# Scores pair by pair of heads, a search traced by an estimate, and decays from rows of sums: one change to a hybrid attention block

## The chip, the cores and the metric

The kernel runs on one core of a Trainium2 chip. The time is that of one execution on the device in microseconds. TensorE multiplies matrices, VectorE, ScalarE and GpSimd work elementwise, and SyncE issues the transfers. PSUM is the memory into which TensorE accumulates.

## The reference, cut to what matters

One residual block over 1024 rows of 1024 columns: a mixer of two parallel head groups, one output projection, and an MLP. One input projection makes everything that the mixer needs.

```python
def hybrid_mixer(h, w_in, ...):
    proj = h @ w_in
    q_a, c_kv, q_idx, k_idx, w_idx, q_b, k_b, v_b, a_b, b_b, z_b = jnp.split(proj, ...)
    o_a = dsa_mixer(q_a, c_kv, q_idx, k_idx, w_idx, ...)
    o_b = gated_deltanet_mixer(q_b, k_b, v_b, a_b, b_b, z_b, ...)
    return jnp.concatenate([o_a, o_b], axis=-1) @ w_out

# dsa_mixer, for a block of 128 rows: 8 index heads score all keys, the 256 best are kept
    rel = jax.nn.relu(jnp.einsum('bqhd,bsd->bqhs', qi_b, k_idx))
    score = jnp.einsum('bqhs,bqh->bqs', rel, wi_b)
    score = jnp.where(key_pos < limit, score, -jnp.inf)
    _, idx = lax.top_k(score, topk)

# gated delta rule, for a chunk of 64 rows, one of 4 heads
    g = jnp.cumsum(chunks(g), axis=-1)
    decay = jnp.exp(jnp.where(causal, g[..., :, None] - g[..., None, :], -jnp.inf))
    lower = jnp.where(strict, jnp.einsum('bhncd,bhnsd->bhncs', k_beta, k) * decay, 0.0)
    intra = jnp.where(causal, jnp.einsum('bhncd,bhnsd->bhncs', q, k) * decay, 0.0)
```

## The kernel before

The input projection is a loop over 26 tiles of 128 columns. Each is 48 matmuls: two halves of 512 rows, eight slices of the inner sum, and three products of a high and a low part (lines L199, L200, L201). The columns come in this order: keys and weights of the index heads (kw), four tiles of index queries (qi, a pair of heads in each), then keys and queries of the delta heads in turn (kb, qb), vb, z, the latents c and the attention's queries (qa). A tile's result in PSUM is called two.

What follows a tile is in `projections()`. Behind kw come the gates of the delta rule and, for each of eight blocks of 128 rows, `decays(n)`: two matmuls that sum the gates' logarithms, one exponential, a triangle on GpSimd, and a write to memory (tile tmp, tensor e_d). Behind the fourth qi come the scores, block after block. For each slice of at most 512 keys and each of 8 heads, two matmuls (L480, L481) go to a PSUM bank called tr or ch, ScalarE takes the relu (L486), and VectorE adds it, weighted, to the tile score (L484, L487). Only blocks 7 to 2 are scored: the first two blocks have no more than 256 keys.

The search for the 256th best score, `bisect()`, is 32 steps of counting how many scores lie below a candidate, three blocks on VectorE (L527) and three on ScalarE (L521), with small operations between (L530 to L532). Then masks are made on VectorE (L569 to L577, tile maskb). The convolutions of kb, qb and vb are three multiply-adds on VectorE each (L587, tile tmp). `delta_head(h)` builds the triangular systems of a head (last product L701, tile la). The latents are normalized by two products (L451, L452, tile c_row), turned by TensorE and copied (L1096, tile CT). The attention also needs the up-projection as a split copy (L1088, tile UK).

The order is made by a planner, `Flow`. It holds generators and estimates when each engine and each ring of buffers is free; a generator yields the time or the event that it waits for, and the one that can go on earliest issues next. The search is no part of it in the kernel before: `projections()` advances it by a fixed number of steps after each tile (the table rate). Every engine works through its own queue in the order of issue.

Of the kernel before, what the change touches and what calls it, by code (L numbers as in the profile page):

```python
# [8 lines left out]
F32 = mybir.dt.float32  # L9
# [130 lines left out]
def block_kernel(ctx: ExitStack, tc: tile.TileContext, x, w_in, c_norm, w_uk, w_uv, rel_bias, conv_w, a_log,  # L140
# [98 lines left out]
    after_r = pl.t(dc, [P, P], F32R, "after_r")  # L239
# [49 lines left out]
    warmr = pl.t(px, [P, 1024], F32R, "warmr")  # L289
    V.memset(warmr.bitcast(F32), 0.0)  # L290
    ps = psw()
    for _ in range(10):
        PE.matmul(ps[:, 0:512], warm[:, 0:P], warm, start=True, stop=True)
    ps = psw()
    two = warmr[:, 0:512].rearrange("p (a b) -> p b a", a=2)
    forms = [(warmr[:, 0:P], two), (warmr[:, 0:P], warmr[:, 0:512].rearrange("p (a b) -> p b a", a=4)),
             (warmr[:, 0:256:2], two), (warmr[:, 0:P], warmr[:, 0:256].rearrange("p (a b) -> p b a", a=2))]
    for lhs, rhs in forms:
        o = ps[:, 0:rhs.shape[1] * rhs.shape[2]].rearrange("p (a b) -> p a b", b=rhs.shape[2])
        for _ in range(4):  # L300
            PE.matmul(o, lhs, rhs, start=True, stop=True)
    for _ in range(4):
        for r in range(2):
            rs = slice(64 * r, 64 * r + 64)
            PE.matmul(ps[:, 512 * r:512 * r + 512].rearrange("p (b a) -> p b a", a=2), warmr[rs, 0:P], two[rs],
                      start=True, stop=True)
# [65 lines left out]
    la_d = pl.t(dram, [P, NB * 4, 2, P], F32, "la_d")  # L372
    e_d = pl.t(dram, [4, P, NB, P], F32, "e_d")
# [101 lines left out]
    def scores(b):  # L475
        for s0, w in cuts(P * (b + 1)):
            dst = score[:, soff[b] + s0:soff[b] + s0 + w]
            for h in range(8):
                ps = psx()
                PE.matmul(ps[:, :w], QS[:, h, b * P:(b + 1) * P], KH[:, s0:s0 + w], start=True, stop=False)  # L480
                PE.matmul(ps[:, :w], QS[:, h, b * P:(b + 1) * P], KL[:, s0:s0 + w], start=False, stop=True)  # L481
                wh = wab[:, b, h:h + 1]
                if h == 0:
                    V.tensor_scalar(dst, ps[:, :w], 0.0, wh, op0=OP.max, op1=OP.mult)  # L484
                else:
                    S.activation(ps[:, :w], ps[:, :w], AF.Relu)  # L486
                    V.scalar_tensor_tensor(dst, ps[:, :w], wh, dst, op0=OP.mult, op1=OP.add)  # L487
        G.memset(score[0:64, soff[b] + P * b + 64:soff[b] + P * (b + 1)], PAD)
# [8 lines left out]
    def bisect():  # L497

# [17 lines left out]
        for bit in range(31, -1, -1):  # L516
            flip = (1 << bit) ^ (1 << (bit - 1)) if bit else 1
            for i, b in enumerate(ACB):
                n = P * (b + 1)
                junk = pl.t(ph, [P, T], BF16, "jk", bufs=2)  # L520
                S.activation(junk[:, :n], s_of(b), AF.Sign, bias=cand[:, 3 + i:4 + i].bitcast(F32), scale=-1.0,  # L521
                             accum_out=cnt[:, 3 + i:4 + i])
            for i, b in enumerate(DVB):
                n = P * (b + 1)
                junk = pl.t(ph, [P, T], BF16, "pre")
# [12 lines left out]
            yield  # L538
# [6 lines left out]
        for i, b in enumerate(ACB):  # L545
# [8 lines left out]
            yield  # L554
# [5 lines left out]
        for b in range(NB - 1, 1, -1):  # L560
# [17 lines left out]
            yield  # L578
# [41 lines left out]
    gpr = pl.t(keep, [P, 2, NB, 4], F32R, "gp")  # L620
    gp = gpr.bitcast(F32)

    def gates():
# [32 lines left out]

    def decays(n):

        ps = psx()
        gms = pl.t(ph, [P, 2, 4, P], F32R, "tmp", bufs=4)  # L660
        for i in range(2):
            gm = gms[:, i]
# [287 lines left out]
    def projections():  # L950
        nonlocal dna, dn, dn_close
        for i, (kind, p) in enumerate(plan):
# [19 lines left out]
            if kind == "kw":  # L972
# [3 lines left out]
                for n in range(NB):  # L976
                    decays(n)
# [824 lines left out]
```

## Time and profile before

| | |
|---|---|
| time, median of 3 runs (lowest to highest) | 1409.54 us (1406.29 to 1410.04) |
| profiled execution | 1411.07 us, span 1409.4 us |
| granted TensorE clock, mean | 0.955 |
| TensorE, VectorE, ScalarE, GpSimd busy | 1298.3, 1104.0, 729.7, 271.1 us |

The span is the profiled execution from its first to its last instruction on the core. Busy time counts what an engine executes and not its waits for another. In rows, x2 behind an operation means two of them in one row, an arrow `<-` in brackets names what ended the idle time ahead of an instruction, and L201 is line 201 of the kernel of that run. The profile's shares are means over stages with different limits, so the stages are read one by one.

### The profile page before, as it was taken

To read this page: it belongs to the slowest core of one execution; us is meant where nothing else is said; L and a number is where in the kernel's file an instruction comes from. 1 tells how busy PE (TensorE), PEld (TensorE's weight loads), DVE (VectorE), ACT (ScalarE), POOL (GpSimd) and SP (SyncE) were. 2 spreads that over 40 slices of the span, in tenths; PEclk is the share of its full clock that TensorE was granted. 3 is DMA by queue.
4 is the path that set the end of the run, shared out by engine and by line. 5 is a ranking of instruction groups with operands and counts; after the bars stand their busy time and mean duration, and the time that the engine had idled before them with its cause. 6 is when DMAs were issued, how large, how long until landed. Compare 5 with 4: busy or idle time off the path is not lost.

```text
span 1409.4 us, 20293 instructions
## 1 busy us (share of the span) xinstructions
PE 1298.3 (92%) x6643; PEld 1119.7 (79%) x6643; DVE 1104.0 (78%) x2551; ACT 729.7 (52%) x1521; POOL 271.1 (19%) x296
## 2 busy tenths in 40 slices
PE   7898997998886999999899889999999799999995
PEld 4687895777675799997788778888888688888884
DVE  5524668999999698898777387777777987878886
ACT  4333336768651577677546456565566332343422
POOL 3154221121215345337410000000000000000023
PEclk7999998999995799999999999999999999999998
DMA  6133112456225433333456744555556966646215
GB/s 192 47 97 82 30 46 60 120 149 162 63 70 139 135 89 97 103 110 123 124 171 200 260 158 179 210 206 203 199 206 234 379 237 240 233 126 217 76 50 175
DMA packets 183523, 211.24 MB, mean 150 GB/s; under 512 B 28081, under 2 KB 123514, under 8 KB 183290
## 3 DMA queue, kind: packets, MB, share of 16 engines
q1 hardware_dynamic: 183418, 209.94, 46.2%
q8 instruction: 53, 0.87, 0.3%
q14 instruction: 52, 0.43, 0.1%
HBM read 136.48 MB, written 74.99 MB: 150 GB/s over the span
## 4 chain that ended last, share of the span: by engine, by line
PE 66%; DVE 19%; DMA 6%; ACT 5%; issue 2%; SPq 1%; DVEq 0%; ACTq 0%
PE ch L201 4%; PE sc L199 4%; PE acc L200 4%; PE acc L199 4%; PE sc L201 4%; PE sc L200 4%; PE ch L199 4%; PE acc L201 4%; PE ch L200 4%; PE two L199 4%; PE two L200 4%; PE two L201 4%; DVE pre L527 2%; PE tr L199 2%; PE tr L200 2%
## 5 line engine op out<-in xcount | busy, mean ns | idle before, releaser
L199 PE MATMUL two<-hTH,wh 128*128 128x512 f32 (+1 forms) x416 | 166.9, 403 | 26.0 <-ACT tmp L424 16.0
L200 PE MATMUL two<-hTL,wh 128*128 128x512 f32 (+1 forms) x416 | 166.3, 400 | 0.0
L201 PE MATMUL two<-hTH,wl 128*128 128x512 f32 (+1 forms) x416 | 165.4, 398 | 0.0
L1759 POOL TENSOR_TENSOR tmp<-acc,c_row 128x512 f32<-128x512 f32 x16 | 20.7, 1301 | 635.2 <-DVE acc L1772 626.4
L199 PEld LDWEIGHTS two<-hTH,wh 128*128 128x128 f32 (+1 forms) x416 | 82.3, 198 | 43.3 <-issue 22.6
L521 ACT ACTIVATE jk<-score,cand 128x1024 bf16<-128x1024 f32 (+2 forms) x96 | 92.4, 964 | 45.0 <-DVE cand L532 26.8
L201 PEld LDWEIGHTS two<-hTH,wl 128*128 128x128 f32 (+1 forms) x416 | 81.9, 197 | 12.8 <-issue 1.0
L200 PEld LDWEIGHTS two<-hTL,wh 128*128 128x128 f32 (+1 forms) x416 | 81.9, 197 | 12.3 <-issue 0.7
L1422 ACT CAST hl<-raw 128x512 fp32r<-128x512 f32 x81 | 48.5, 614 | 72.9 <-PE acc L200 48.0
L1422 ACT CAST hl<-tt 128x512 fp32r<-128x512 f32 x56 | 34.4, 617 | 72.6 <-PE tr L200 44.3
L270 POOL TENSOR_TENSOR wl<-stg,wh 128x1024 fp32r<-128x1024 f32 (+1 forms) x26 | 60.8, 2340 | 55.5 <-ACT wh L267 54.0
L1422 ACT CAST hl<-tmp 128x512 fp32r<-128x512 f32 x60 | 35.8, 617 | 55.8 <-DVE tmp L1539 30.4
L1423 DVE TENSOR_TENSOR hl<-raw,hl 128x512 fp32r<-128x512 f32 x81 | 55.7, 692 | 6.3 <-PE acc L201 3.4
L1158 ACT ACTIVATE big<-big,nm 128x256 f32<-128x256 f32 (+6 forms) x64 | 50.6, 791 | 13.5 <-DVE nm L1157 13.5
L269 POOL TENSOR_SCALAR wh<-stg 128x1024 fp32r<-128x1024 f32 x19 | 20.1, 1058 | 190.4 <-PE two L200 190.4
L1183 ACT CAST part<-tr 128x512 fp32r<-128x512 f32 x80 | 43.2, 543 | 21.9 <-PE tr L1181 18.3
L1184 DVE TENSOR_TENSOR part<-tr,part 128x512 fp32r<-128x512 f32 x80 | 50.3, 631 | 4.8 <-ACT part L1183 4.4
L1206 PE MATMUL acc<-part,VS 128*128 128x256 f32 x288 | 49.4, 295 | 1.3 <-DVE part L1184 1.0
L1134 POOL TENSOR_TENSOR mt<-tz,maskb 128x256 f32<-128x256 f32 x56 | 37.8, 679 | 60.2 <-DVE mx L1150 39.7
L587 DVE SCALAR_TENSOR_TENSOR tmp<-two,svT,tmp 128x1023 f32<-128x1023 f32 (+2 forms) x36 | 45.5, 1276 | 4.1 <-ACT tmp L585 3.0
L199 PE MATMUL sc<-hl,hq 128*128 128x512 f32 x112 | 43.3, 386 | 5.2 <-DMA hq<-hid 2.4
L201 PE MATMUL ch<-h2H,hl 128*128 128x512 f32 x112 | 43.6, 390 | 3.6 <-DVE hl L1423 3.6
(516 smaller groups left out, 4159.2 us busy)
## 6 DMA issues: line engine op xcount, KB each, us to landing
hid<-tmp SPq DMA_DIRECT2D x140, 256.0 KB, 2.3
hq<-hid SPq DMA_DIRECT2D x80, 256.0 KB, 5.2
raw<-in_w_mlp_in_dram SPq DMA_DIRECT2D x14, 1024.0 KB, 5.5
tmp<-hid SPq DMA_DIRECT2D x56, 256.0 KB, 5.3
raw<-in_w_mlp_out_dram SPq DMA_DIRECT2D x13, 1024.0 KB, 8.5
stg<-in_w_in_dram SPq DMA_DIRECT2D x25, 512.0 KB, 4.0
x<-in_x_dram SPq DMA_DIRECT2D x8, 512.0 KB, 5.3
la_d<-la SPq DMA_DIRECT2D x8, 512.0 KB, 3.7
```

Source lines behind the costliest of these rows:

```text
L199: PE.matmul(o, lh, rh, start=start, stop=False, skip_group_check=more)
L200: PE.matmul(o, lh, rl, start=False, stop=False, skip_group_check=more)
L201: PE.matmul(o, ll, rh, start=False, stop=stop, skip_group_check=more)
L270: G.tensor_sub(wl[:, :, :n], f[:, :, :n], wh[:, :, :n].bitcast(F32))
L521: S.activation(junk[:, :n], s_of(b), AF.Sign, bias=cand[:, 3 + i:4 + i].bitcast(F32), scale=-1.0, accum_out=cnt[:, 3 + i:4 + i])
L587: V.scalar_tensor_tensor(acc[:, 3 - j:T], both[:, 0:T - 3 + j], w[j], acc[:, 3 - j:T], op0=OP.mult, op1=OP.add)
L1158: S.activation(pr[:, :n], pr[:, :n], AF.Exp, bias=nm, accum_out=den[:, hh:hh + 1])
L1183: S.copy(pt[:, 0:2 * nj, 0, :], v4(ps)[:, 0:2 * nj])
L1184: V.tensor_sub(pt[:, 0:2 * nj, 1, :], v4(ps)[:, 0:2 * nj], pt[:, 0:2 * nj, 0, :].bitcast(F32))
L1206: PE.matmul(po[:, hh * 256:hh * 256 + 256], VS[:, j + a, 2 * p + hh, :], pt[:, 2 * a + hh].rearrange("p a t -> p (a t)"), start=j + a + hh ...
L1422: S.copy(h_, src)
L1423: eng.tensor_sub(l_, src, h_.bitcast(F32))
```

## The change

It has four parts.

- The warm-up of TensorE before the first transposes is 34 matmuls of one kind in place of 10 of that kind and 24 of four other forms.
- The scores become a generator of the planner, `scoring()`. It goes pair by pair of heads, as each qi tile is done, and over all blocks for that pair, and waits for an estimated free PSUM bank. The low part of a block's last columns is filled behind all scores.
- The search becomes a generator too, which begins at the event "scored" and yields an estimate of each step's time; the table of rates goes. The other generators' estimates are changed with it.
- The decays: the gates' running sums (32 columns, a block and head each) are copied, negated (ng), transposed on TensorE to 32 rows, and written to memory (g_d). For two blocks at a time one transfer spreads eight rows of g_d to all 128 partitions, GpSimd puts -1e30 outside the triangle, and ScalarE takes eight exponentials of 128 columns each, with the negated sum as its bias. The four calls stand behind the first kb tile and the first qb tile and not behind kw.

```diff
     ps = psw()
-    for _ in range(10):
+    for _ in range(34):
         PE.matmul(ps[:, 0:512], warm[:, 0:P], warm, start=True, stop=True)
...
-    def scores(b):
-        for s0, w in cuts(P * (b + 1)):
-            dst = score[:, soff[b] + s0:soff[b] + s0 + w]
-            for h in range(8):
...
+    def scoring():
+        for p in range(4):
+            yield ("qi", p)
+            for b in range(NB - 1, 1, -1):
+                for s0, w in cuts(P * (b + 1)):
+                    dst = score[:, soff[b] + s0:soff[b] + s0 + w]
+                    for h in (2 * p, 2 * p + 1):
+                        while flow.bank("px", 4) > flow.now:
+                            yield flow.bank("px", 4)
+                        ps = psx()
...
+                        t = flow.pe(2 * w / 2260)
...
+                        flow.took("px", dve(t, w / 960 + 0.16))
+                        yield 0.0
...
+        flow.done("scored", flow.rings["px"][-1])
...
     def bisect():
+        yield "scored"
...
+            ta = td = flow.now
...
+                ta = act(ta, n / 1200 + 0.45)
...
+                td = dve(td, n / 960 + 0.28)
...
-            yield
+            yield dve(max(ta, td), 0.8)
...
-        S.copy(gpr[:, 0], g)
-        V.tensor_sub(gpr[:, 1], g, gp[:, 0])
-        S.copy(after_r, after)
...
+        V.tensor_copy(gs, ps[:, 0:32])
+        V.tensor_scalar(sm("ng", (P, 32)), gs, -1.0, None, op0=OP.mult)
+        PE.transpose(ps[0:32, 128:256], gs, ident)
+        gt = pl.t(ph, [32, P], F32, "gt")
+        V.tensor_copy(gt, ps[0:32, 128:256])
+        SY.dma_start(g_d, gt)
 
     def decays(n):
-        for i in range(2):
-            gm = gms[:, i]
-            G.tensor_tensor(gm, upto[:, None, :].to_broadcast(H4), b4(gp[:, i, n, :]), OP.mult)
-            PE.matmul(ps, after_r, gm.rearrange("p h c -> p (h c)"), start=i == 0, stop=i == 1)
-        S.activation(e, v4(ps), AF.Exp)
-        G.affine_select(e, e, pattern=[[0, 4], [1, P]], compare_op=OP.is_ge, fill=0.0, base=0, channel_multiplier=-1)
-        SY.dma_start(e_d[:, :, n, :].rearrange("h s c -> s h c"), e)
+        e = tmp4()
+        src = g_d[4 * n:4 * n + 8, :]
+        SY.dma_start(e, bass.AP(tensor=src.tensor, offset=src.offset, ap=[[0, P], [1, T]]))
+        G.affine_select(e3, e3, pattern=[[0, 8], [1, P]], compare_op=OP.is_ge, fill=-1e30, base=0,
+                        channel_multiplier=-1)
+        for i in range(8):
+            S.activation(e[:, cs], e[:, cs], AF.Exp, bias=sm("ng", (P, 32))[:, 4 * n + i:4 * n + i + 1])
+        for i in range(2):
+            SY.dma_start(e_d[:, :, n + i, :].rearrange("h s c -> s h c"), e3[:, 4 * i:4 * i + 4])
...
-                for n in range(NB):
-                    decays(n)
-            elif (kind, p) == ("qi", 3):
-                for b in range(NB - 1, 1, -1):
-                    scores(b)
...
-            for _ in range(rate.get(kind, 0)):
-                next(topk, None)
...
-    for rank, gen in enumerate((chain(), levels(0), levels(1), emits(), projections())):
+    for rank, gen in enumerate((chain(), levels(0), levels(1), emits(), scoring(), bisect(), projections())):
```

TensorE's queue around the first score. In the kernel before it stands behind 305 matmuls of projections (L199 to L201), in the seventh tile, next to the last decay (L664); ident, hTH, hTL, wh and wl are operands of transposes and projections, KH, KL and QS the split keys and the queries of the index heads:

```order
L199 MATMUL two_1384<-hTH_108,wh_820 128x512
L200 MATMUL two_1384<-hTL_109,wh_820 128x512
L664 MATMUL tr_611<-tmp_612,after_r_84 128x512
L480 MATMUL tr_883<-KH_377,QS_376 128x512
L481 MATMUL tr_883<-KL_378,QS_376 128x512
L201 MATMUL two_1384<-hTH_108,wl_821 128x512
```

In the changed kernel the scores' matmuls are L471 and L472, and the first two pairs stand behind 120 of the projections:

```order
L200 MATMUL two_621<-hTL_108,wh_391 128x512
L201 MATMUL two_621<-hTH_107,wl_392 128x512
L471 MATMUL ch_641<-KH_374,QS_373 128x512
L472 MATMUL ch_641<-KL_375,QS_373 128x512
L471 MATMUL ch_650<-KH_374,QS_373 128x512
L472 MATMUL ch_650<-KL_375,QS_373 128x512
L199 MATMUL two_774<-hTH_107,wh_552 128x512
```

What moved: the first score, from the seventh tile to the end of the second tile's first half. The last score stands behind 624 projection matmuls before, and behind 524 in the changed kernel.

ScalarE's queue where the decays' exponentials begin. Before, one of them (L666) stands between copies of the index queries (L409) and a split copy of weights (L267):

```order
L409 ACTIVATE QS_376<-two_763 64x512
L666 ACTIVATE tmp_557<-tr_551 128x512
L409 ACTIVATE QS_376<-two_763 64x512
L267 CAST wh_757<-stg_759 128x1024
L409 ACTIVATE QS_376<-two_700 64x512
```

In the changed kernel (copies L394, relus of the scores L478, exponentials L671, x8 is eight in a row):

```order
L478 ACTIVATE ch_674<-ch_674 128x448
L394 ACTIVATE QS_373<-two_621 64x512
L394 ACTIVATE QS_373<-two_774 64x512
L671 ACTIVATE tmp_1288<-tmp_1288,sm_ng_501 128x128 x8
L478 ACTIVATE ch_686<-ch_686 128x384
L671 ACTIVATE tmp_1303<-tmp_1303,sm_ng_501 128x128 x8
L478 ACTIVATE ch_702<-ch_702 128x384
```

What moved: the exponentials come in groups of eight, and relus of scores stand between and behind them.

VectorE's queue where the latents are normalized. Before, both products stand among steps of the search (L527, L530) and products of the triangular systems (L720, L721):

```order
L451 TENSOR_TENSOR c_row_355<-c_row_355,cr_y_3223 128x1024
L527 TENSOR_SCALAR pre_3274,cnt_1347<-score_372,cand_1345 128x896
L530 TENSOR_SCALAR bare_1346<-cand_1345 128x6
L721 TENSOR_TENSOR kqh_2242<-kqh_2242,kqh_2247 128x6x26
L452 TENSOR_TENSOR c_row_355<-c_row_355,cn_b_3199 128x1024
```

In the changed kernel they (L436, L437) stand behind the last mask (L578), and behind the small steps of a reciprocal root (L215 to L217):

```order
L578 TENSOR_SCALAR maskb_352<-jk_3635 128x384
L215 SCALAR_TENSOR_TENSOR cr_u_2941<-cr_y_2940 128x8
L216 TENSOR_TENSOR cr_u_2941<-cr_u_2941,css_2918 128x8
L217 SCALAR_TENSOR_TENSOR cr_y_2940<-cr_u_2941,cr_y_2940 128x8
L436 TENSOR_TENSOR c_row_351<-c_row_351,cr_y_2940 128x1024
L437 TENSOR_TENSOR c_row_351<-c_row_351,cn_b_2916 128x1024
```

What moved: the normalization, from the middle of the search to the end of the masks. Between the last score and the fourth delta head's last row, VectorE's queue holds 21 operations of convolutions (L587) in place of 18, and 16 of each of the search's small operations in place of 17; TensorE's holds 341 to 365 projection matmuls in place of 312.

## Rows read from the trace of the kernel before

**Rows 1.** The page: busy time of three engines (share of the span, instructions), and the chain that ended last by engine.

```profile
PE 1298.3 (92%) x6643; PEld 1119.7 (79%) x6643; DVE 1104.0 (78%) x2551; ACT 729.7 (52%) x1521; POOL 271.1 (19%) x296
...
PE 66%; DVE 19%; DMA 6%; ACT 5%; issue 2%; SPq 1%; DVEq 0%; ACTq 0%
```

**Rows 2.** Busy time by stretch: the stretch and its length, then busy us (and instructions) of TensorE, its weight loads, VectorE, ScalarE and GpSimd, the granted clock, and the share and rate of transfers.

```profile
0.00:70.70 70.70, 54.26 (x229) 37.98 (x229) 39.56 (x75) 31.34 (x51) 16.99 (x63) 0.83 0.41 119
70.70:115.80 45.10, 44.76 (x209) 38.74 (x208) 11.01 (x21) 15.24 (x25) 29.11 (x26) 1.00 0.34 92
115.80:230.00 114.20, 107.79 (x492) 89.79 (x490) 74.24 (x102) 50.12 (x90) 29.49 (x26) 0.97 0.19 50
230.00:341.90 111.90, 95.28 (x429) 80.11 (x428) 108.52 (x297) 80.73 (x158) 22.26 (x16) 0.92 0.43 123
341.90:457.20 115.30, 90.13 (x404) 76.86 (x404) 110.21 (x268) 56.74 (x128) 32.90 (x20) 0.83 0.41 106
457.20:676.00 218.80, 210.06 (x1627) 191.10 (x1628) 188.88 (x719) 154.17 (x408) 101.45 (x114) 0.96 0.36 108
```

**Rows 3.** Timeline of TensorE: the 119th and 120th matmul of the projections. Columns here and below: start, duration, engine, line, operation, out<-in, shape, count, and idle time ahead with its releaser.

```profile
70.48 0.38 PE L200 MATMUL two<-hTL,wh 128*128 128x512 f32 x1
70.70 0.38 PE L201 MATMUL two<-hTH,wl 128*128 128x512 f32 x1
```

**Rows 4.** Timeline of TensorE around the first score.

```profile
114.03 0.38 PE L200 MATMUL two<-hTL,wh 128*128 128x512 f32 x1
114.25 0.38 PE L201 MATMUL two<-hTH,wl 128*128 128x512 f32 x1
114.46 0.38 PE L199 MATMUL two<-hTH,wh 128*128 128x512 f32 x1
114.68 0.38 PE L200 MATMUL two<-hTL,wh 128*128 128x512 f32 x1
114.89 0.40 PE L664 MATMUL tr<-tmp,after_r 128*128 128x512 f32 x1
115.13 0.40 PE L480 MATMUL tr<-KH,QS 128*128 128x512 f32 x1
115.37 0.40 PE L481 MATMUL tr<-KL,QS 128*128 128x512 f32 x1
```

**Rows 5.** Timelines of VectorE: the last weighted score, the last row of the fourth delta head, the last mask.

```profile
229.42 0.62 DVE L487 SCALAR_TENSOR_TENSOR score<-ch,wab,score 128x384 f32<-128x384 f32 x1
...
341.44 0.47 DVE L701 SCALAR_TENSOR_TENSOR la<-ch,sm_f,eh 128x256 f32<-128x256 f32 x1
...
456.26 0.93 DVE L577 TENSOR_SCALAR maskb<-jk 128x384 bf16<-128x384 bf16 x1
```

**Rows 6.** Waits: engine, tile and line that waited <- what released it, then us in total, times, longest. The first two are VectorE's from 70.7 to 229.5 us, the last two TensorE's from 229.5 to 341.5 us.

```profile
DVE QS L410 <- ACT QS L409: 27.8, 10, 10.1
DVE score L487 <- ACT ch L486: 23.6, 17, 6.5
...
PE tr L700 <- DVE la L701: 6.6, 3, 3.3
PE two L199 <- DVE tmp L587: 3.7, 1, 3.7
```

**Rows 7.** The decays' operations by line (duration in ns: least, median, most; first and last start), the landing of their writes, the exponential of the gates' sums, a 128-column activation of the attention, and two transfers of 512 KB on the page (KB each, median us from issue to landing).

```profile
L666 ACT ACTIVATE tmp<-tr x4: 578/590/597, 78.3 to 116.5; 128x512 f32<-128x512 f32 x4
...
L663 POOL TENSOR_TENSOR tmp<-upto,gp x16: 1033/1040/1054, 73.4 to 117.0; 128x512 fp32r<-128x512 f32 x16
...
L667 POOL TENSOR_SCALAR_AFFINE_SELECT tmp<-tmp x8: 628/634/647, 78.9 to 123.7; 128x512 f32<-128x512 f32 x8
...
DMA to landing us min/median/max: 2.3/2.3/4.1
...
76.38 0.25 ACT L655 ACTIVATE sm_eg<-tr 128x96 f32<-128x96 f32 x1 [0.66 <-PE tr L653]
...
462.56 0.30 ACT L923 ACTIVATE sq<-o 128x128 bf16<-128x128 f32 x1
...
stg<-in_w_in_dram SPq DMA_DIRECT2D x25, 512.0 KB, 4.0
...
x<-in_x_dram SPq DMA_DIRECT2D x8, 512.0 KB, 5.3
```

**Rows 8.** The page: the convolutions' multiply-adds (busy us, mean ns of one | idle ahead of them).

```profile
L587 DVE SCALAR_TENSOR_TENSOR tmp<-two,svT,tmp 128x1023 f32<-128x1023 f32 (+2 forms) x36 | 45.5, 1276 | 4.1 <-ACT tmp L585 3.0
```

**Rows 9.** Timelines: the latents' normalization on VectorE, then ScalarE's copies of the latents and of the up-projection.

```profile
401.35 1.21 DVE L451 TENSOR_TENSOR c_row<-c_row,cr_y 128x1024 f32<-128x1024 f32 x1
...
403.86 1.22 DVE L452 TENSOR_TENSOR c_row<-c_row,cn_b 128x1024 f32<-128x1024 f32 x1
...
456.32 1.07 ACT L1096 CAST CT<-tr 128x512 fp32r<-128x512 f32 x2 [3.33 <-DVE jk L576]
...
464.00 0.61 ACT L1088 CAST UK<-big 128x512 fp32r<-128x512 f32 x1
```

More of the change, by code (lines that the diff above doesn't have):

```diff
@@ L473, in bias @@
         SY.dma_start(tz_d, src)
-    def scores(b):
-        for s0, w in cuts(P * (b + 1)):
-            dst = score[:, soff[b] + s0:soff[b] + s0 + w]
-            for h in range(8):
[L479 to L488, printed above, removed]
+    def scoring():
[8 more added lines that the diff above has]
+                        ps = psx()
+                        PE.matmul(ps[:, :w], QS[:, h, b * P:(b + 1) * P], KH[:, s0:s0 + w], start=True, stop=False)
+                        PE.matmul(ps[:, :w], QS[:, h, b * P:(b + 1) * P], KL[:, s0:s0 + w], start=False, stop=True)
+                        wh = wab[:, b, h:h + 1]
+                        t = flow.pe(2 * w / 2260)
+                        if h == 0:
+                            V.tensor_scalar(dst, ps[:, :w], 0.0, wh, op0=OP.max, op1=OP.mult)
+                        else:
+                            S.activation(ps[:, :w], ps[:, :w], AF.Relu)
+                            V.scalar_tensor_tensor(dst, ps[:, :w], wh, dst, op0=OP.mult, op1=OP.add)
+                            t = act(t, w / 1200 + 0.18)
+                        flow.took("px", dve(t, w / 960 + 0.16))
+                        yield 0.0
+        for b in range(NB - 1, 1, -1):
+            G.memset(score[0:64, soff[b] + P * b + 64:soff[b] + P * (b + 1)], PAD)
+        flow.done("scored", flow.rings["px"][-1])
     DVB, ACB = [6, 3, 2], [7, 5, 4]
@@ L577, in bisect @@
             V.tensor_scalar(maskb[:, moff[b]:moff[b] + n], eq[:, :n], -NEG, NEG, op0=OP.mult, op1=OP.add)
-            yield
+            yield dve(act(flow.now, n / 1200 + 0.4), 5.5 * n / 960 + 1.0)
+        flow.done("topk", flow.now)
     def conv(both, blk, dst, keep_in=None):
@@ L986, in projections @@
                     conv(loaded["both"], blk, v_d[:, :, p, :])
+                    act(dve(act(flow.now, 1.05), 3.7), 1.1)
                 else:
+                    act(dve(act(flow.now, 1.05), 3.7), 1.1)
+                    if p == 0:
+                        for n in range(4 * (kind == "qb"), 4 + 4 * (kind == "qb"), 2):
+                            decays(n)
+                    if kind == "qb" and p == 0:
+                        yield "scored"
+                        pi_close()
+                        dna, dna_close = pl.open("dna", side="right")
                     if kind == "kb":
```

42 lines of the change are left out of this document (11 added, 31 removed).

## The prediction

> **What bounds the kernel now.** I read the page's busy shares first, then the same shares stage by stage, then the single instructions at the borders of the stages. Over the whole span TensorE is busy 92% and VectorE 78%, and the chain that ended last is two thirds TensorE and a fifth VectorE [rows 1]. That is a mean over stages with different limits, and the change touches only the first third. So I cut the span where the work that the change moves begins and ends [rows 2]. From 70.7 to 115.8 us TensorE is busy 44.76 of 45.1 us with projections and decays, and VectorE only 11.01: it has nearly nothing to do. From 115.8 to 230.0 us the scores of the search run: TensorE 107.79 of 114.2, VectorE 74.24. From there to the last mask VectorE is busy 108.52 of 111.9 and 110.21 of 115.3 us, 97% and 96%, and TensorE has 16.6 and 25.2 us to spare. So the kernel is bound by TensorE up to the last score, and by VectorE from the last score to the last mask; attention (457.2 to 676) is bound by TensorE again, 210 of 219 us. What this asks of the change is clear: what makes the last score come earlier lets the long VectorE stretch (search, convolutions, delta heads, masks) start earlier; what only removes TensorE work behind the last score gives nothing.
>
> Where the last score falls is set by how much of TensorE's queue stands ahead of it. In the trace the first score matmul starts at 115.13 [rows 4] and the last weighted sum of a score at 229.42; the fourth delta head's last row starts at 341.44 and the last mask at 456.26 [rows 5].
>
> **The change part by part.**
>
> *Warm-up.* 34 matmuls replace 34 of other kinds at the very start. The first border that I time is at 70.7 us, and up to there TensorE is busy only 54 of 70.7 us [rows 2], waiting for loads and norms. A few us more or less at the head are covered by that. 0, bounds -1.5 and +1.5.
>
> *Scores pair by pair.* By the order of TensorE's queue, 305 projection matmuls stood ahead of the first score and 624 ahead of the last; now it is 120 and 524. The 120th is the one that starts at 70.70 [rows 3], so the stretch from there to the last score loses 100 projection matmuls. Four starts in a row at 114.03 to 114.68 give 0.217 us for one [rows 4]: 21.7 us. The same stretch loses the 16 decay matmuls, 0.24 us each from 114.89 to 115.13: 3.8 us. The 160 score matmuls and VectorE's 80 sums stay. TensorE sets this stretch (152.6 of 159.3 us), so the last score comes 25.5 us earlier, at 204 us, if TensorE's idle time in it stays as it is. Idle it was 6.7 us [rows 2]; VectorE in the same stretch waited for ScalarE's relu and for ScalarE's query copies, 23.6 and 27.8 us [rows 6], which says that the path through relu and sum is not full. If the idle time goes, and the granted clock, 0.97 in the scores, comes back to 1.0, the last score is some 10 us earlier still; if the pair-wise order doubles the waits, 10 us later. -25.5, bounds -36 and -15.
>
> *Decays.* They leave TensorE and its accumulators and go to SyncE's transfers, GpSimd and ScalarE. Before, ScalarE did 8 exponentials of 512 columns at 0.59 us: 4.7 us [rows 7]. Now it does 32 of 128 columns; the nearest row is a 128-column activation, 0.3 us: 9.6 us. GpSimd gives up 16 products of 1.04 us and 8 selections of 0.63 and does 4 selections of twice the size, about 5 us instead of 21.7. ScalarE is busy 15.24 + 50.12 of 159.3 us there, so 4.9 us more do not make it the bound. But its queue is in order, and the exponentials stand among the relus that the scores wait for. What the first of them waits for can be timed: the sums leave TensorE at about 76.4 (the exponential of the same sums [rows 7]), copies and transpose take about 1 us, the write of the sums lands 2.3 us after its issue (the decays' own write is the row), the spread to 128 partitions 4.0 to 5.3 us after that (loads of 512 KB), and GpSimd's selection takes 1.3: 85 to 86.5 us. In ScalarE's new queue they stand behind the query copies of the 168th projection matmul, with 5 pairs of score matmuls ahead: 70.7 + 48 x 0.217 + 10 x 0.24 = 83.5. So ScalarE waits 1.5 to 3 us here, and about as much can happen at the second group. TensorE has projections between its scores to cover part of it. +2, bounds 0 and +8.
>
> The row of ScalarE shows the 128-column form at half the time of the 512-column form, for a quarter of the work. The Trainium skill, "Advanced Engine Details and Errata", section "The Read-Write Bubble", says why: on ScalarE and VectorE the memory latency shows between instructions, so tiles of 512 or 1024 elements are better; it speaks against this part. The trace agrees (0.30 against 0.59 us), and by either it is some 5 us on an engine that is not the bound here.
>
> *From the last score to the last row of the fourth delta head.* This stretch, 111.9 us long, is VectorE's. By the order, one convolution more stands in it (three sums of 1.28 us [rows 8], 3.8 us) and one step's three small operations less (0.5 us): +3.3. TensorE gets 29 to 53 of the postponed projection matmuls here (341 to 365 instead of 312), 6.3 to 11.5 us; it had 16.6 us to spare, but it also waited 6.6 us for the delta heads' products on VectorE and 3.7 for a convolution [rows 6], so the two engines hold each other up a little more. I take +6, nearer the lower end, since VectorE has at most 3% to lose; bounds +3 and +12.
>
> *To the end of the masks.* The work is the same but for the normalization of the latents: its two products of 1.2 us were done at 401 to 405 [rows 9], and now stand behind the last mask. Counted through, VectorE's last operation of the stretch comes 1.3 us later than without. Cover: the latents are copied at 456.32, but the keys need the up-projection, which is copied only at 464.00. With that cover the end moves by 0 to 2, without it by 3 to 5. +1.5.
>
> *Attention and the MLP.* The same instructions; in attention some stand in another order. 0, bounds -4 and +4.
>
> **The sum.** 0 - 25.5 + 2 + 6 + 1.5 + 0 = -16. Against the profiled execution (1411.07 us with a span of 1409.4) this is 1395; the median of the runs, 1409.54, lies 1.5 below it, so I forecast **1394 us**. What a measurement of this kernel can tell from no change is about 0.3%, 4.2 us.
>
> **The rivals.**
>
> *The gain is eaten behind the scores.* The 100 matmuls are only postponed. If TensorE keeps all its idle time in the two later stretches, they add 100 x 0.217 = 21.7 us there, and -25.5 + 2 + 21.7 + 1.5 gives 1408 to 1410: no change. For it: the waits between TensorE and VectorE in both directions [rows 6]. Against: 41.8 us of idle TensorE in the 227 us behind the scores.
>
> *More is won.* VectorE's stretch starts at 194 instead of 204, because the scores no longer come in one dense block at the end, and the later stretches stay VectorE's own length (+3.3, 0): -36 + 0 + 3.3 = -33, which gives 1377. For it: VectorE's 11 of 45 us before the first score. Against: TensorE at 94% in the scores already.
>
> *Slower: ScalarE stands still.* The exponentials wait for two transfers in a row and a selection, with the relus of the scores behind them, and the score banks fill until TensorE stops. Each wait costs TensorE what it exceeds the work between two scores. It becomes slower than before when the two groups together cost over 20 us, say 10 each, which asks for a spread that lands 15 us after its issue rather than 5; the weight loads stand behind the decays' writes on SyncE, so a late group also delays a projection's weights (load 4.0 us). At 15 us each the time would be about 1422. For it: the tail of the queue on SyncE; a write of these decays took 4.1 us at most [rows 7]. Against: all loads of this size land within 5.3.
>
> The Trainium skill, "DMA: Bandwidth & Descriptors", section "Anatomy of one DMA", gives about 2.0 us of fixed cost to each transfer (for those that GpSimd issues; these come from SyncE). The shortest row here, 2.3 us, agrees; two transfers in a row would be 4 us by it, inside the 6.3 to 7.6 that I counted.
>
> **How the numbers follow.** My forecast (a gain of 8 to 24 us) has 0.55, the eaten gain 0.18, more won 0.15, ScalarE's wait or a worse order of attention 0.12. Leaving out the far part of the last and the farthest part of the third gives 1375 to 1411. Of the eaten gain about a fifth is still faster by 4.2 us; so faster 0.74, same 0.15, slower 0.11.
>
> **What would show it.** In the trace after: the first score at 71 us, the last weighted sum at 200 to 208; VectorE above 95% from there to the last mask, which starts at 436 to 446; ScalarE's first 128-column exponential at 84 to 88 us with a wait of a few us ahead of it; TensorE above 93% from 71 us to the last score. The forecast is wrong if the last score is early and the last mask is not (the eaten gain), if ScalarE waits over 10 us for the selections, or if attention, 219 us before, differs by more than 4.

## The result, and the profile after

The changed kernel takes 1390.39 us (median of 4 runs, 1387.90 to 1392.46), the kernel before beside it 1408.91. The ratio is 0.987 (95% interval 0.985 to 0.989): 18.5 us faster. The profiled execution has a span of 1386.2 us. It is the fastest of the four, and the profiled execution before (1411.07 us) was slower than its median, so the stages below add up to 23 us and not to 18.5.

The same stages as in [rows 2], now cut at the changed kernel's own borders (first score, last weighted score, fourth delta head, last mask). Columns as there.

```profile
0.00:67.80 67.80, 52.60 (x229) 34.76 (x229) 39.04 (x75) 31.69 (x50) 17.01 (x63) 0.87 0.42 127
67.80:194.10 126.30, 123.72 (x581) 106.86 (x582) 79.01 (x120) 66.68 (x137) 31.56 (x25) 0.99 0.27 79
194.10:309.90 115.80, 106.88 (x499) 91.05 (x498) 111.14 (x297) 79.70 (x152) 29.13 (x21) 0.97 0.45 132
309.90:427.10 117.20, 90.85 (x415) 77.58 (x413) 112.74 (x264) 59.61 (x132) 34.57 (x21) 0.87 0.39 103
```

The stretch with the scores is 126.3 us long (126.8 from the 120th projection matmul, where it was 159.3), with TensorE busy 98% of it. VectorE is as dense as before in the two stretches behind, 96% each, and they are 3.9 and 1.9 us longer. The borders in the timelines of TensorE, VectorE and ScalarE (answering to [rows 3 to 5] and [rows 9]):

```profile
67.18 0.38 PE L201 MATMUL two<-hTH,wl 128*128 128x512 f32 x1
67.81 0.50 PE L471 MATMUL ch<-KH,QS 128*128 128x512 f32 x1 [0.25 <-DVE QS L395]
...
309.29 0.47 DVE L706 SCALAR_TENSOR_TENSOR la<-ch,sm_f,eh 128x256 f32<-128x256 f32 x1
...
426.67 0.25 DVE L578 TENSOR_SCALAR maskb<-jk 128x384 bf16<-128x384 bf16 x1
...
429.35 1.23 DVE L437 TENSOR_TENSOR c_row<-c_row,cn_b 128x1024 f32<-128x1024 f32 x1
...
433.64 0.62 ACT L1092 CAST UK<-big 128x512 fp32r<-128x512 f32 x1
```

The 120th projection matmul starts at 67.18, the first score behind it. The last mask starts at 426.67 and not at 456.26. The latents' normalization ends 3.7 us behind the mask's end; the latents' copies end at 434.0, the up-projection's at 434.3.

ScalarE at the decays' exponentials, where the slower rival would have shown:

```profile
84.78 0.59 ACT L394 ACTIVATE QS<-two 64x512 fp32r<-64x512 f32 x1 [0.84 <-DVE QS L395]
85.40 2.45 ACT L671 ACTIVATE tmp<-tmp,sm_ng 128x128 f32<-128x128 f32 x8
87.87 0.47 ACT L478 ACTIVATE ch<-ch 128x384 f32<-128x384 f32 x1
```

No idle time stands ahead of them. GpSimd's first selection started at 83.9 and took 1.1 us, so it ended 0.4 us before ScalarE came to the exponentials.

Of 30 us at the last mask, 23 are left at the end. From the last logits (690.3 before, 661.5 after) to the last split copy ahead of the MLP it took 105.9 us before and 112.0 after. In that stretch TensorE stood idle 5.4 us, where it was 1.7. It waited once for a small operation of VectorE (r) ahead of a matmul into the output projection's bank sc, and once for a split copy (ol), which it had not before:

```profile
PE sc L199 <- DVE r L217: 3.1, 1, 3.1
PE sc L201 <- DVE ol L1308: 1.8, 1, 1.8
```

### The profile page after: what moved, and what is told of

The parts are those of the page before. It is cut to its first block, busy times and chain, and to the rows that moved or that the text cites. A ratio compares the mean times of both kernels' runs of the same rounds, so it can differ in the third digit from the quotient of the medians.

```text
span 1386.2 us, 20222 instructions
## 1 busy us (share of the span) xinstructions
PE 1284.0 (93%) x6628; PEld 1110.4 (80%) x6628; DVE 1108.2 (80%) x2552; ACT 735.4 (53%) x1543; POOL 253.7 (18%) x276
## 4 chain that ended last, share of the span: by engine, by line
PE 65%; DVE 19%; DMA 7%; ACT 5%; issue 2%; POOL 0%; SPq 0%; DVEq 0%; ACTq 0%
PE sc L199 4%; PE sc L200 4%; PE sc L201 4%; PE ch L201 4%; PE ch L199 4%; PE ch L200 4%; PE acc L199 4%; PE acc L200 4%; PE acc L201 4%; DVE pre L528 3%; PE two L199 3%; PE two L200 3%; PE two L201 3%; PE tr L199 2%; PE tr L201 2%
## 5 line engine op out<-in xcount | busy, mean ns | idle before, releaser
L199 PE MATMUL two<-hTH,wh 128*128 128x512 f32 (+1 forms) x416 | 164.5, 398 | 23.0 <-ACT tmp L409 10.6
L201 PE MATMUL two<-hTH,wl 128*128 128x512 f32 (+1 forms) x416 | 162.0, 391 | 0.0
L1763 POOL TENSOR_TENSOR tmp<-acc,c_row 128x512 f32<-128x512 f32 x16 | 20.7, 1301 | 644.1 <-DVE acc L1776 632.5
L199 PEld LDWEIGHTS two<-hTH,wh 128*128 128x128 f32 (+1 forms) x416 | 80.6, 194 | 38.9 <-issue 19.7
L201 PEld LDWEIGHTS two<-hTH,wl 128*128 128x128 f32 (+1 forms) x416 | 80.1, 193 | 12.0 <-issue 0.5
L199 PE MATMUL acc<-h2H,hl 128*128 128x512 f32 x120 | 46.3, 387 | 1.6 <-ACT tmp L1477 1.6
L1185 PE MATMUL tr<-ident,big 128*128 128x128 f32 x288 | 46.7, 277 | 0.5 <-DVE part L1188 0.4
```

Of the source, the lines that this page charges most:

```text
L199: PE.matmul(o, lh, rh, start=start, stop=False, skip_group_check=more)
L201: PE.matmul(o, ll, rh, start=False, stop=stop, skip_group_check=more)
L1185: PE.transpose(ps[:, c * P:(c + 1) * P], u["p"][hh][:, (j + a) * P:(j + a + 1) * P], ident)
```

## The experiments

Times are medians; the kernel before, run beside each set, was 1409.0, 1407.6, 1409.8 and 1407.6 us. The borders come from each kernel's profiled execution (us). The logits are the attention's products of queries and keys (TensorE, bank sc); attention here is the time from the first to the last of them. Chain means the matmuls of the delta rule's chain that stand ahead of the first logits in TensorE's queue, without those that go through one helper: eight more in every kernel but the one with the search by the table, which has none there. Lean means that one product of three is left out in some tiles.

| kernel | last score ends | last mask ends | first, last logits | chain | time |
|---|---|---|---|---|---|
| before | 230.0 | 457.2 | 475.6, 690.3 | 68 | 1408.9 |
| changed | 194.0 | 426.9 | 443.1, 661.5 | 64 | 1390.4 |
| new decays alone | 216.0 | 437.9 | 454.7, 681.0 | 44 | 1403.3 |
| changed, old decays | 227.2 | 448.1 | 477.8, 696.3 | 64 | 1418.4 |
| changed, old warm-up | 196.1 | 429.0 | 446.0, 662.5 | 64 | 1389.1 |
| changed, pairs behind the fourth qi | 212.2 | 437.9 | 456.1, 672.8 | 64 | 1399.3 |
| changed, search by the table | 196.3 | 427.9 | 441.3, 666.6 | 44 | 1388.4 |
| changed, lean behind the last score | 198.1 | 433.0 | 452.2, 666.2 | 56 | 1385.5 |
| changed, lean ahead of it | 197.4 | 422.6 | 440.7, 655.6 | 64 | 1383.2 |
| changed, three more transfers | 195.3 | 425.3 | 451.0, 670.2 | 64 | 1398.7 |
| changed, latents ahead of z | 194.8 | 431.2 | 450.3, 662.4 | 68 | 1382.4 |
| changed, latents ahead of vb | 194.3 | 434.4 | 455.6, 666.2 | 76 | 1385.6 |
| new decays alone, BASE 75 | 214.7 | 430.8 | 457.9, 668.5 | 76 | 1390.0 |
| before, BASE 75 | 228.1 | 452.4 | 478.4, 688.1 | 76 | 1409.8 |

**The new decays alone.**

```diff
# the kernel before, with the new end of gates() and the new decays(n)
+        SY.dma_start(g_d, gt)
...
-                for n in range(NB):
-                    decays(n)
...
+                    if p == 0:
+                        for n in range(4 * (kind == "qb"), 4 + 4 * (kind == "qb"), 2):
+                            decays(n)
```

> The kernel before with the new decays alone (gates' sums written and spread by transfers, behind the first kb and qb tile). In TensorE's queue the first score then stands behind 144 projection matmuls instead of 305, since no decay holds a bank ahead of it; the last one still stands behind 624. Theory A (the place of the last score in the queue sets the end): only the 16 decay matmuls leave, 3.8 us, so about 1405. Theory B (what counts is that the scores start early, because the dense tail of scores from 215 to 229 us goes): the last score comes at about 215 and the time is about 1395.

1403.33 us, ratio 0.997 (0.995 to 0.999): 5.7 us faster. The last score came at 216, 14 us earlier, as B had it, and the last mask 19 us earlier; but the end gained only 6 (8 between the profiled executions). So B is right on the scores and A seems right on the time, for another reason: attention takes 226.3 us instead of 214.7, and from the last mask to the last logits pass 243.1 us instead of 233.1. That gap led to the runs with BASE below.

Of the 14 us, 2 lie ahead of the 120th projection matmul (68.52 here, 70.70 before). From there to the last score it is 147.5 us instead of 159.3:

```profile
68.50:216.00 147.50, 144.94 (x685) 124.83 (x683) 84.65 (x125) 70.46 (x138) 42.17 (x31) 1.00 0.29 82
```

**The old decays in the changed kernel.**

```diff
# the changed kernel, with the old gates() and the old decays(n)
...
+                for n in range(NB):
+                    decays(n)
...
-                    if p == 0:
-                        for n in range(4 * (kind == "qb"), 4 + 4 * (kind == "qb"), 2):
-                            decays(n)
```

> The changed kernel with the old decays back (two matmuls in a bank of the scores' ring each, behind kw); pair-by-pair scores, search and warm-up stay. In the queue the scores now stand where they stood in the kernel before: first behind 305 projection matmuls, last behind 624. Theory A (place of the last score): no gain there, 1405 to 1409. Rival (the search's estimates and the order of pairs carry the gain, and the decays only free 4 us): about 1394.

1418.42 us, ratio 1.007 (1.004 to 1.010): slower than the kernel before. TensorE's timeline at the first score:

```profile
111.94 0.38 PE L200 MATMUL two<-hTL,wh 128*128 128x512 f32 x1
112.16 0.40 PE L666 MATMUL tr<-tmp,after_r 128*128 128x512 f32 x1
112.39 0.40 PE L471 MATMUL tr<-KH,QS 128*128 128x512 f32 x1
```

The pair-wise generator is there, and yet the first score stands right behind a decay's first matmul (L666), as in [rows 4]. In both kernels that is the seventh decay of eight, not the last: scores and decays take their banks from one ring in turn, a tr and then a ch, and the seventh is the last decay in a tr. The first score in a ch stands right behind the eighth. So it was in the kernel before, with GpSimd's products for the eighth decay ahead of it:

```profile
116.02 2.04 POOL L663 TENSOR_TENSOR tmp<-upto,gp 128x512 fp32r<-128x512 f32 x2
...
121.51 0.39 PE L664 MATMUL ch<-tmp,after_r 128*128 128x512 f32 x1
121.73 0.40 PE L480 MATMUL ch<-KH,QS 128*128 128x512 f32 x1
```

In both kernels no score goes ahead of a decay whose bank comes earlier in the ring, and the decays' matmuls come behind their products on GpSimd. From the 120th projection matmul to the last score's end it is 159.3 us with the pairs and the old decays, the same 159.3 as before. What moved the first score is the decays, not the generator. The new decays take no bank of this ring, and they are also called later, behind the first kb tile; no run tells the two apart. That this kernel is even slower, outside both ranges, comes from behind the masks, which are 9 us earlier than before: its latents' normalization ends 16 us behind them, and from the last mask to the last logits pass 248.2 us instead of 233.1.

**The old warm-up.**

```diff
# the changed kernel
-    for _ in range(34):
+    for _ in range(10):
...
```

> The changed kernel with the old warm-up of TensorE. In the profile of the changed kernel the first score came 3.5 us before my forecast because the stretch at the lower clock lay at 20 to 25 us and not at 27 to 32. Theory: the warm-up's last matmuls set when that stretch comes, so 3 to 4 us are lost, about 1394. Rival: it lies by chance, and the time stays at 1390.

1389.14 us (1385.63 to 1393.34), 1.3 us below the changed kernel, with overlapping runs: the rival. The first score lay at 69.9 us here; in other kernels with the new warm-up and the early pairs it lay at 67.8 to 71.5, so the new warm-up does not fix it.

**Pairs, but only behind the fourth tile of queries.**

```diff
# the changed kernel
-            yield ("qi", p)
+            yield ("qi", 3)
```

> The changed kernel, but the generator of scores waits for the fourth tile of index queries before its first pair; the order by pairs stays. In TensorE's queue the first score stands behind 144 projection matmuls and the last behind 624 (changed kernel: 120 and 520). Theory A (place of the last score): the last score comes 104 x 0.217 = 22.6 us later, of which the stretches behind give back 4 to 7 us, so 1405 to 1410. Theory B (the early start is what counts): within 4 us of the changed kernel, 1390 to 1395.

1399.27 us, ratio 0.993 (0.991 to 0.995). The last score came 18.2 us later than in the changed kernel, near A's 22.6, and the time 8.9 us later, between the two ranges. Some half of what the last score loses is given back behind; the last mask is 11.0 us later. Where that comes from is said behind the two lean kernels below.

**The search by the old table.**

```diff
# the changed kernel; bisect() is no longer one of the planner's generators
+    topk = bisect()
+    rate = {"kb": 1, "qb": 1, "vb": 2, "z": 3, "c": 3, "qa": 3}
...
-        yield "topk"
+            for _ in range(rate.get(kind, 0)):
+                next(topk, None)
+        for _ in topk:
+            pass
...
```

> The changed kernel with the search advanced by the old table of steps after each tile and not by an estimate. Theory (the search's estimate is worth nothing, since VectorE's queue is full either way): 1388 to 1393. Rival: with the table only 44 matmuls of the delta rule's chain stand ahead of the first logits in TensorE's queue instead of 64, and they come back in attention, which TensorE bounds: 5 us slower, about 1395.

1388.38 us (1385.98 to 1391.71): the theory. The rival's mechanism is there, and is paid back: attention takes 225.3 us instead of 218.4, but the first logits come 1.8 us earlier, and the output projection behind takes 108 us instead of 112.

**One product of three left out, behind and ahead of the last score.**

```diff
# the changed kernel, in mm3, for tiles 12 to 26 or for tiles 6 to 11
-        PE.matmul(o, lh, rl, start=False, stop=False, skip_group_check=more)
+        if not lean:
+            PE.matmul(o, lh, rl, start=False, stop=False, skip_group_check=more)
```

> The changed kernel that leaves out one of the three products in the projection tiles 12 to 26, nearly all behind the last score: 240 matmuls, 52 us of TensorE; the order stays. Theory (VectorE bounds the stretch from the last score to the masks): the last score stays, the last mask comes at most 6 us earlier (what the two engines hold each other up), 1384 to 1390. Rival (TensorE sets it as much, so that postponed matmuls cost what they take): the last mask comes 15 us or more earlier, below 1376.

1385.51 us. From the last score to the last mask's end (busy time of the stretch, first of this kernel, then of the changed kernel):

```profile
198.00:432.80 234.80, 149.00 (x684) 125.43 (x683) 222.03 (x567) 139.69 (x287) 64.78 (x43) 0.81 0.42 115
```

```profile
194.10:427.10 233.00, 197.73 (x912) 168.64 (x910) 223.89 (x560) 139.31 (x284) 63.70 (x42) 0.92 0.42 117
```

TensorE has 49 us less to do, and the stretch is 1.8 us longer, with VectorE's busy time nearly the same. VectorE sets it; the postponed matmuls cost nothing there. (The planner's order did not stay quite the same: 56 of the chain's matmuls stand ahead of the logits, and the fourth delta head ended 12.7 us later.)

> The changed kernel that leaves out one of the three products in the projection tiles 6 to 11, which stand ahead of the last score: 96 matmuls, 20.8 us of TensorE. Theory (TensorE bounds the stretch of the scores): the last score comes 18 to 21 us earlier and the time falls by 14 to 21, to 1369 to 1376. Rival (relu and sum of the scores on ScalarE and VectorE are the next bound at once): the last score gains under 10 us, 1380 to 1386.

1383.24 us, in the rival's range, and the last score ended at 197.4, no earlier than in the changed kernel. This did not test what it was meant to: with shorter tiles the queue took in later tiles ahead of the last score, which stands behind 528 projection matmuls instead of 520. Nearly the same count gave nearly the same time; whether relu and sum would be the next bound is open. The gain lies behind: from the last score to the last mask 225.2 us, 7.7 fewer than in the changed kernel. TensorE has 20 us less to do there, but VectorE also has 8.4 us less. With the pairs behind the fourth qi it is much the same. First this kernel, then that one:

```profile
197.40:422.60 225.20, 178.21 (x811) 151.03 (x808) 215.42 (x556) 137.53 (x282) 51.54 (x36) 0.88 0.43 117
```

```profile
212.20:437.90 225.70, 178.51 (x808) 151.00 (x808) 216.66 (x556) 137.65 (x283) 53.00 (x34) 0.88 0.42 117
```

The profiles of all fourteen kernels agree on this stretch: it is as long as VectorE's busy time in it (208 to 227 us) and 7 to 14 us more, while TensorE's busy time goes from 149 to 203 us. So what is given back behind a later last score is VectorE's work: with the pairs behind the fourth qi, 3.6 us more of it lies ahead of the last score than in the changed kernel and 3.4 us more between the last mask and the last logits.

**Three more transfers ahead of the spread.**

```diff
# the changed kernel
-        SY.dma_start(g_d, gt)
+        SY.dma_start(g1_d, gt)
+        SY.dma_start(g2_d, g1_d)
+        SY.dma_start(g3_d, g2_d)
+        SY.dma_start(g_d, g3_d)
```

> The changed kernel with three more transfers in a row between the write of the gates' sums and their spread. In the profile of the changed kernel ScalarE reached the first exponentials at 85.40, 0.4 us after GpSimd's selection ended, so it did not wait. Three more transfers at 1.4 to 2.3 us put the selection's end 4 to 7 us later. Theory: ScalarE waits 4 to 7 us at the first group only, TensorE covers half, and the time is 1390 to 1394. Rival (relus behind the exponentials stop the scores at once): the last score comes as much later as ScalarE waits, and more, over 1395.

1398.66 us, 8.3 us over the changed kernel. ScalarE's wait (from 80 to 145 us):

```profile
ACT tmp L677 <- POOL tmp L673: 4.0, 3, 2.5
```

It waited 4.0 us in all. The first score came 1.5 us later than in the changed kernel, the last one 1.3 us later and the last mask 1.6 us earlier, so this wait cost the scores nothing. But the queue's order changed with it: the two relus that stood behind the first two groups now stand ahead of them, and a long wait with relus behind it was not tried. The 8 us arose behind: the latents' normalization ended at 437.9, 13 us behind the masks, and the first logits came 7.9 us later. The time is the rival's, the mechanism is not.

**The latents earlier.**

```diff
# the changed kernel, with the latents ahead of z
-    plan += [("vb", p) for p in range(4)] + [("z", p) for p in range(4)] + [("c", 0)] + [("qa", p) for p in range(4)]
+    plan += [("vb", p) for p in range(4)] + [("c", 0)] + [("z", p) for p in range(4)] + [("qa", p) for p in range(4)]
# ... and ahead of vb
+    plan += [("c", 0)] + [("vb", p) for p in range(4)] + [("z", p) for p in range(4)] + [("qa", p) for p in range(4)]
```

> The changed kernel with the latents' tile (c) projected ahead of the four z tiles. In VectorE's queue the normalization of the latents then stands long before the masks instead of 3.6 us behind the last of them. Theory: in the changed kernel TensorE waited 7.2 us for it ahead of turning the latents, but the up-projection's copy is ready only at 433.6 to 434.4 against 434.1 for the latents, so at most 1 to 3 us come back: 1387 to 1389. Rival: the copy of the up-projection moves too, since ScalarE is free, and 4 to 7 us come back, 1383 to 1386.

> The changed kernel with the latents' tile ahead of the vb tiles, one place further forward than ahead of the z tiles (1382.4). 76 matmuls of the delta rule's chain stand ahead of the first logits (changed kernel 64, latents ahead of z 68). Theory (what the latents' early tile brought is that the chain's matmuls fill TensorE's wait for the masks): 1379 to 1383. Rival (it was the order of the output projection, which a plan meets by chance): anywhere from 1382 to 1392.

Ahead of z: 1382.38 us (1381.59 to 1386.97), ratio to before 0.983 (0.980 to 0.985), the lowest median of this study. Ahead of vb: 1385.62 (1384.04 to 1391.91); the runs of the two overlap. Neither of my reasons holds for the first: its first logits come later, at 450.3 instead of 443.1, its last logits 0.9 us later, and the gain lies behind them, 106.7 us instead of 112.0 to the last split copy ahead of the MLP, near the 105.9 before the change. In the second, 76 of the chain's matmuls are ahead of the logits and attention is 210.6 us, but the logits begin 12.5 us later than in the changed kernel. It fits the rival (an order that a plan meets or misses), which is not shown by that; why just these orders of the output projection are better I can't say.

**The planner's estimate of the triangular systems.**

```diff
# the kernel before, with the new decays and then without them
-    BASE = 90.0
+    BASE = 75.0
```

> The kernel before with the new decays alone, and one more number changed: the planner's estimate of when the triangular systems are ready (BASE) is 75 us and not 90. In TensorE's queue 76 matmuls of the delta rule's chain then stand ahead of the first logits; with the new decays alone they were 44, in the kernel before 68. Theory (the new decays bring the masks 19 us earlier, but of that 13 were lost because matmuls of the chain, which had filled TensorE's wait for the masks, moved into attention, which TensorE bounds): attention gets shorter by 8 to 13 us and the time is 1392 to 1397. Rival (attention is longer for its own order, and the chain has nothing to do with it): within 3 us of the new decays alone, 1400 to 1406.

1389.96 us (1386.85 to 1395.04), ratio 0.987 (0.984 to 0.990), a little below the theory's range. Attention by busy time, with the new decays alone and then with BASE at 75:

```profile
455.00:681.20 226.20, 211.56 (x1651) 192.03 (x1650) 201.17 (x729) 152.12 (x405) 105.83 (x119) 0.98 0.33 100
```

```profile
458.00:668.50 210.50, 203.21 (x1590) 185.47 (x1591) 185.10 (x709) 151.18 (x403) 105.15 (x118) 1.00 0.35 107
```

TensorE has 8.4 us less to do in attention, VectorE 16.1 us less, and it is 15.7 us shorter. But the first logits also come 3.2 us later, and the last mask 7.1 us earlier, so the 15.7 us are not what was won. Between the two profiled executions, 16.2 us apart, 7.1 lie ahead of the last mask, 5.4 from there to the last logits (237.7 us instead of 243.1), and 3.7 behind. Only the 5.4 can be the chain's that the theory means.

The table shows the same in all kernels. With 44 of the chain's matmuls ahead of the logits attention takes 225 and 226 us, with 56 to 68 212 to 219, with 76 210 to 211. From the last mask to the last logits, where the later start counts too, it is 239 and 243 us with 44, 231 to 248 with 56 to 68, and 232 to 238 with 76. So the chain's place shifts time between the wait and attention; how much of it reaches the end these kernels don't show.

> The kernel before with one number changed: the planner's estimate BASE is 75 us and not 90; the old decays and scores stay. 76 matmuls of the delta rule's chain stand ahead of the first logits and not 68; the last score stays behind 624 projection matmuls, so the last score stays at 230 us and the masks near 457. Theory (the 13 us that the same number brought beside the new decays were the 19 us that the masks had been early and attention had lost): without earlier masks there is little to bring, 1403 to 1408. Rival (the number is worth 13 us by itself, and the decays 6): about 1396.

1409.75 us, ratio 1.0015 (0.9996 to 1.0034): nothing, and just above the theory's range, though the last mask came 4.8 us earlier than in the kernel before (in the profiled executions). So the 13 us are not the number's by itself; that it pays only where the masks come early fits both kernels and is not shown by them. And the new decays with that estimate, without pairs, without the planner's search and without the new warm-up, are as fast as the whole change.

## Why the prediction was right, and where its steps were not

The time (1394 forecast, 1390.4 measured) and the frame were right: TensorE sets the stretch up to the last score, VectorE the one behind it, and leaving out 49 us of TensorE behind the last score did not shorten that. The steps between fit less well: the first score (67.8 us), the last weighted sum (193.4) and the last mask (426.7) all came earlier than the times that were to show the forecast (71, 200 to 208, 436 to 446). Term by term, in the profiled executions:

- *Warm-up*, 0: the 120th matmul started 3.5 us before the forecast's border, at 67.18. The old warm-up gave the same time, the kernel before with BASE at 75 has the old warm-up and its 120th at 67.35, and lean behind the last score has the new one and its 120th at 70.90, so the warm-up does not set this. The gain of 3.5 us is outside the term's bounds and luck; that the warm-up is worth nothing was right.
- *Scores and waits of ScalarE*, -23.5: measured 126.8 instead of 159.3 us, -32.5. It is mis-sized by 9 us, near the end of its bounds. Of these, 3.9 are TensorE's idle time, which I kept at 6.7 us and of which 2.8 were left; 2.0 are the wait of ScalarE that did not come; and 3.1 are busy time of TensorE, of which 0.9 is a miscount: 520 projection matmuls stand ahead of the last score in the trace, not 524. The rest of the 3.1 I can't place.
- *Who moves the first score.* I put the 185 places that it gained down to the generator of pairs, and gave the decays 3.8 us. That step failed. In the queue, 161 of the 185 places are there with the new decays alone, and with the old decays the pairs gained nothing. From the 120th projection matmul to the last score's end, 159.3 us before, the new decays alone save 11.9 us, the pairs with the old decays none, and the pairs beside the new decays 20.7 more. So the price of the pairs' places (21.7) was near, but it is paid only once the decays are out of the way, and theirs was three times what I gave. The decays held the banks of the scores' ring, which I could have read from [rows 4], where the first score stands right behind a decay, and from ScalarE's wait for decays from 70 to 130 us:

```profile
ACT tmp L666 <- PE tr L664: 12.3, 2, 7.3
```

- *To the fourth delta head*, +6: +3.9. *To the last mask*, +1.5: +1.9, with the latents' 3.7 us behind covered by the up-projection's copy, as forecast.
- *Attention and what follows*, 0 with 4 either way: +7.6, outside my bounds. From the last mask to the last logits 1.5 us were lost and from there to the MLP 6.1. Neither instructions nor sizes changed, only the planner's order. This is the term that kept the time near the forecast when the scores gained 9 us more than I had given them.

So the number was right in part by luck: errors of opposite sign cancelled, 12.5 us too little up to the last score against 7.6 too much behind the masks, and the attribution to the parts was wrong. Up to the last mask the trace follows the rival that more is won: VectorE's stretch starts at 194.0, as it had it, and the last mask comes 30 us earlier, near its 33. Its reason, that the scores no longer come in one dense block, was not tested. The eaten gain was a good rival in kind: of the 36 us at the last score 13 are gone at the end. But 5.8 of them went to VectorE's own work in its stretch (5.2 us more busy time than before), not to TensorE, and 7.6 behind the masks.

The slower rival did not come about: ScalarE did not wait at all. The write of the sums landed after 1.4 us, less than either price that I had for a transfer (2.0 and 2.3), and from its issue to the first selection's start passed 5.8 us, less than the 6.3 to 7.6 that I counted (the 4 us of the prediction lie below these, not inside); and ScalarE came to the exponentials at 85.4 and not at 83.5. With three more transfers it waited 4.0 us and the scores lost nothing; a wait of the 15 us that this rival asks for was not tried.

## What to carry to other kernels

Before a gain is credited to a new order of issue, ask what else stands in the same ring of banks: an operation that waits for another engine and takes its slot in turn can hold everything behind it, whatever the order asks for. Test the parts of a change in both directions, each alone on the old kernel and each taken out of the new one: here the pairs were worth nothing without the new decays. In a stage that one engine sets, count that engine's own work which moves into it or out of it; here this said how much of an earlier start was kept. And where a planner orders later stages from estimates, give the untouched stages some 0.5% either way (7.6 us here), and try a second plan before judging the change.

## What I had not expected of the hardware

- The changed kernel and its variants with the early pairs had their first score at 67.8 to 71.5 us. In the kernel before the 120th projection matmul started at 70.70, and at 67.35 with BASE at 75, a change that touches nothing ahead of it. In all fourteen profiles the granted clock was 0.50 to 0.60 from 20.2 to 22.2 us, at or near the lower of TensorE's two levels. From 27.6 to 32.3 it was 0.50 in two of them, the kernel before among them, 1.00 in seven, the changed kernel among them, and between these in five. Ahead of that stretch TensorE had stood idle for 3.1 us in the kernel before and for 1.9 in the changed kernel. First the kernel before, then with BASE at 75, then the changed kernel:

```profile
27.50:32.40 4.90, 4.90 (x14) 3.64 (x13) 3.84 (x6) 0.69 (x1) 1.31 (x22) 0.50 0.45 116
```

```profile
27.50:32.40 4.90, 4.90 (x28) 3.98 (x27) 4.52 (x7) 1.63 (x3) 1.34 (x23) 1.00 0.41 118
```

```profile
27.50:32.40 4.90, 4.90 (x28) 3.98 (x27) 4.44 (x7) 1.64 (x3) 1.25 (x21) 1.00 0.47 115
```

- The write of 16 KB of sums landed 1.4 us after its issue, the spreads of 512 KB after 3.8 to 5.3 us.
- With TensorE at 63% instead of 85% between last score and last mask its granted clock was 0.81 instead of 0.92, and the time of that stretch did not show it.
